# A Hymba decoder layer on one core: other step tables, five more seven-product pairs, extra buffers in two parts

## The chip, the core and the metric

The kernel runs on one core of a Trainium2 chip. The metric is the device time of one execution in microseconds (us), less being better. TensorE (PE) multiplies, VectorE (DVE) and ScalarE (ACT) split and add, GpSimd (POOL) does small work and starts some transfers, SyncE (SP) starts most of them.

## The reference

One layer over 256 tokens of width 2048, in float32. The change touches only the last three matrix products:

```python
u = rmsnorm(h, ln1_w)
...                                    # recurrent and retention heads give y
h = h + y @ w_out                      # 2048 x 2048
u = rmsnorm(h, ln2_w)
ff = silu(u @ w_gate) * (u @ w_up)     # 2048 x 5632, twice
h = h + ff @ w_down                    # 5632 x 2048
return rmsnorm(h, final_norm_w)
```

## The kernel before, in words

**Splits.** Every float32 operand is cut into a high part, a cast to float32r on ScalarE (`split`, L123), and a low part, the difference, on VectorE (L124). A product is then three matmuls, high by high, high by low and low by high (`three`, L683 to L685), each 128x128 by 128x512. Weights come by 512 KB transfers on SP's queue into `raw` tiles; the splits of one such tile are the pair `wh`, `wl` (`split_tiles`), or smaller tiles of the common pool (`bh`, `t4h`).

**Pairs.** The depth of a product is walked in pairs of 128-row tiles. A pair against a 512-column part of each side makes a 2x2 by 2x2 block product for a result in four PSUM banks, c11, c12, c21 and c22. A plain pair does it in eight products, 24 matmuls (`EIGHT`). A "summed" pair does it in seven, 21 matmuls, after Winograd: VectorE first forms four sums of the weights (`Quad.add`, L661) and four of the left side (`Left`, L546).

**Blocks.** A block is a 1024-column part of one weight matrix. Blocks 0 and 1 are `w_out`, blocks 2 to 12 are gate and up (eight pairs each), and then come two blocks of down (22 pairs each, d = 0 and 1). In blocks 0 to 12 a summed pair has two parts: the "share" (four products, 12 matmuls, done ahead during the block before, in `Block.share`, into the next block's banks) and the "direct" rest (three products, 9 matmuls, in the block itself, after a second transfer of half the weights, `Direct`). After the last share an epilogue corrects the banks: ScalarE copies c11 (L806), VectorE forms p and q (L807, L808), ScalarE writes q to c12 (L809), VectorE corrects c22 and c21 (L810, L811). Only then may the next block's plain and direct products add to these banks.

**The order of the work** is written by hand, one string per block in `STEPS`: p is a plain pair, h half of one, s a share for the block after, d a direct rest. `SUMMED` lists each block's summed pairs; `SUMMED_DOWN` and `ORDER_DOWN` do so for down, whose first three summed pairs of d = 0 are shared during block 12. A loop at the end (`AHEAD`, L1130) keeps three half-pair loads, with their splits and sums, ahead of the step that uses them. A scheduler then orders the instructions of each engine.

**Seams.** At the end of block 1, `out_post` adds the residual rows to the banks (L597), squares them on ScalarE (L598), and `turn` transposes them on TensorE into four banks (`ht`, L588), which ScalarE scales into `hf` (L591) and splits (`Left`). The rows are saved to DRAM (`kept_rows`) and read back for down, where `down_post` multiplies them by the final norm's weight `fw` (L984) and writes the output.

**Buffers.** There are six `raw` and four split tiles. From block 3 to block 12 the space of the residual rows is lent to two more of each (`raw2`, `split2`); `swap_back` returns it at the start of down and loads the eight rows and `fw` at once on GpSimd's queue.

Of the kernel before, what the change touches and what calls it, by code (L numbers as in the profile page):

```python
# [14 lines left out]
P = 128  # L15
# [27 lines left out]

@with_exitstack
def tile_hymba_layer(ctx: ExitStack, tc: tile.TileContext, A: dict, out: bass.AP):
# [2 lines left out]

    cpool = ctx.enter_context(tc.tile_pool(name="consts", bufs=1))
    apool = ctx.enter_context(tc.tile_pool(name="acts", bufs=60))  # L50
    rpool = ctx.enter_context(tc.tile_pool(name="raw", bufs=6))
    wpool = ctx.enter_context(tc.tile_pool(name="split", bufs=4))
    early = ctx.enter_context(ExitStack())
    xpool = early.enter_context(tc.tile_pool(name="resid", bufs=8))
    epool = early.enter_context(tc.tile_pool(name="conv", bufs=2))
    tpool = early.enter_context(tc.tile_pool(name="tmp", bufs=6))
    late, resid, more, turn_of = [], [xpool], [], [0, 0]
    extra = ExitStack()
# [5 lines left out]
    def nm(s):  # L64
        counter[0] += 1
        return f"{s}_{counter[0]}"

    def act_tile(name, dt=F32):
        return apool.tile([P, 512], dt, tag="act", name=nm(name))
# [2 lines left out]
        return resid[0].tile([P, 512], dt, tag="xh", name=nm(name))  # L72

    def split_tiles():
        turn_of[1] += 1
        pool_ = more[1] if more and turn_of[1] % 3 == 0 else wpool
        return [pool_.tile([P, 1024], F32R, tag=g, name=nm(g)) for g in ("wh", "wl")]

    def raw_tile():
        turn_of[0] += 1  # L80
        pool_ = more[0] if more and turn_of[0] % 4 == 0 else rpool
        return pool_.tile([P, 1024], F32, tag="raw", name=nm("raw"))

    def late_tile(name, dt=F32):
        return late[0].tile([P, 512], dt, tag="late", name=nm(name))
# [40 lines left out]
    class Unit:  # L126
# [113 lines left out]
    def defer(steps, f):  # L240
        later.append([steps, f])
# [305 lines left out]
    class Left:  # L547
# [3 lines left out]

        names = ("a11", "a21", "a12", "a22", "s1", "s2", "s3", "s4")

        def __init__(self, f, sums):
            self.h, self.l = [act_tile("ah", F32R)], [act_tile("al", F32R)]
            split(self.h[0], self.l[0], f)
            if sums:
                a11, a21, a12, a22 = (f[:, n * P : n * P + P] for n in range(4))
                g = act_tile("s")
                s1, s2, s3, s4 = (g[:, n * P : n * P + P] for n in range(4))  # L560
                v.tensor_tensor(out=s1, in0=a22, in1=a21, op=ALU.subtract)
                v.tensor_tensor(out=s2, in0=a11, in1=s1, op=ALU.add)
                v.tensor_tensor(out=s3, in0=a11, in1=a21, op=ALU.subtract)
                v.tensor_tensor(out=s4, in0=a12, in1=s2, op=ALU.subtract)
                self.h.append(act_tile("sh", F32R))
                self.l.append(act_tile("sl", F32R))
                split(self.h[1], self.l[1], g)

        def __getitem__(self, which):
# [117 lines left out]
    def block(index, quads, lefts, post, ps, tail, early={}, ordered=False):  # L687
# [214 lines left out]

    def make_left(p):
        if dl[p] is None:
            dl[p] = Left(ff[p], p in EARLY_DOWN + SUMMED_DOWN[0] + SUMMED_DOWN[1])

    def down_block(d, ahead):
        ps = {} if d else ahead.ps
# [63 lines left out]
    def down_post(cb, t, c0, cw, src=None):  # L972

        h = htok[(cb, t)][:, c0 : c0 + cw]
        src = h if src is None else src
        f = fw[cb][:, c0 : c0 + cw]
# [126 lines left out]
    def stop_more():  # L1103
        more.clear()

    def swap_back():
        extra.close()
        late.append(ctx.enter_context(tc.tile_pool(name="late", bufs=4)))
        resid[0] = ctx.enter_context(tc.tile_pool(name="resid2", bufs=8))
        for key in [(cb, t) for cb in range(4) for t in range(2)]:  # L1110
# [8 lines left out]
    ]  # L1119
    down = Block(NB + 2, lambda i: A["w_down"][i], dl, None, "", EARLY_DOWN, make_left)  # L1120
    for b, after in zip(blocks, blocks[1:] + [down]):
        if b.index == 3:
            program.append(([], swap))
        if b.index == NB + 1:
            program.append(([], stop_more))
        b.put(after)
    program.append(([], swap_back))

    for d in range(2):
        down_block(d, down)  # L1130
# [117 lines left out]
```

## Time and profile before

| | before |
| --- | --- |
| median of three runs | 1083.56 us (1082.75 to 1084.05) |
| the profiled execution | 1082.46 us |
| its span | 1080.7 us (1.76 us lie outside it) |
| TensorE matmuls | 1070.2 us busy, 5089 instructions |
| TensorE weight loads | 897.7 us busy |
| VectorE | 964.1 us busy, 1399 instructions |
| ScalarE | 664.5 us busy, 947 instructions |
| GpSimd | 57.2 us busy, 73 instructions |

Busy times are of the span. A matmul row shows 0.39 us, but matmuls overlap, so what counts is the distance from one start to the next. "Idle before" and the waits name what ended an engine's idle time; idle time of an engine that nobody waits for costs nothing.

### The profile page before, as it was taken

The numbers are of one execution on the slowest core, as the hardware profiler recorded it, in microseconds if no ns is written. First come the engines' busy times: TensorE is split into PE (matmuls) and PEld (weight loads), VectorE is DVE, ScalarE is ACT, GpSimd is POOL, SyncE is SP. The second block draws the span as 40 slices with busy tenths as digits, with TensorE's granted clock in tenths as the row PEclk, the third lists the DMA queues.
The fourth block names the chain that finished last, engine by engine and source line by source line (L and its number), as shares of the span: only waits on it lengthen the run. The fifth ranks groups of instructions, "written<-read, shape, count | busy, mean of one in ns | idle before, by whom it ended". The sixth has DMA issues, their size and how long they took to land.

```text
span 1080.7 us, 14590 instructions
## 1 busy us (share of the span) xinstructions
PE 1070.2 (99%) x5089; PEld 897.7 (83%) x5089; DVE 964.1 (89%) x1399; ACT 664.5 (61%) x947; POOL 57.2 (5%) x73
## 2 busy tenths in 40 slices
PE   9999999999999999999999999999999999999997
PEld 7888888888888888888888888888888888888886
DVE  7889789988878889989999999999999889997886
ACT  7666644468756676656656565665656656654563
POOL 0602230000000000000000000000002000000001
PEclk9999999999999999999999999999999999999999
DMA  9965475554556588677776777777767856474662
GB/s 325 336 213 171 159 254 166 183 176 158 192 195 234 183 304 273 231 235 256 257 270 228 251 260 242 263 269 232 258 234 270 289 181 214 162 245 159 214 212 101
DMA packets 71386, 244.62 MB, mean 226 GB/s; under 512 B 8208, under 2 KB 8592, under 8 KB 71312
## 3 DMA queue, kind: packets, MB, share of 16 engines
q1 hardware_dynamic: 68400, 236.34, 64.6%
q0 software_dynamic: 1472, 4.72, 1.3%
q10 hardware_dynamic: 1440, 2.62, 0.6%
q8 instruction: 40, 0.66, 0.2%
q14 instruction: 34, 0.28, 0.1%
HBM read 239.46 MB, written 4.19 MB: 225 GB/s over the span
## 4 chain that ended last, share of the span: by engine, by line
PE 98%; DVE 1%; DMA 1%; POOL 0%; SPq 0%; ACT 0%; issue 0%; POOLq 0%; ACTq 0%
PE c L685 22%; PE c L683 22%; PE c L684 22%; PE fm L194 11%; PE fm L196 5%; PE tm L174 3%; PE tm L175 3%; PE tm L176 3%; PE p L683 1%; PE p L685 1%; PE p L684 1%; PE ft L865 1%; DMA x<-in_x 1%; PE ht L588 0%; PE sc L492 0%; DVE wl L124 0%
## 5 line engine op out<-in xcount | busy, mean ns | idle before, releaser
L123 ACT CAST wh<-raw 128x1024 fp32r<-128x1024 f32 (+1 forms) x498 | 462.9, 959 | 323.8 <-PE c L685 130.8
L124 DVE TENSOR_TENSOR wl<-raw,wh 128x1024 fp32r<-128x1024 f32 (+1 forms) x498 | 542.2, 1115 | 72.5 <-ACT wh L123 71.2
L684 PE MATMUL c<-wl,ah 128*128 128x512 f32 x826 | 322.7, 391 | 0.0
L685 PE MATMUL c<-wh,al 128*128 128x512 f32 x826 | 321.8, 390 | 0.0
L683 PE MATMUL c<-wh,ah 128*128 128x512 f32 x826 | 280.3, 391 | 0.0
L683 PEld LDWEIGHTS c<-wh,ah 128*128 128x128 f32 x826 | 155.1, 188 | 32.0 <-ACT wh L123 0.3
L685 PEld LDWEIGHTS c<-wh,al 128*128 128x128 f32 x826 | 155.2, 188 | 31.8
L684 PEld LDWEIGHTS c<-wl,ah 128*128 128x128 f32 x826 | 155.2, 188 | 31.6
L194 PE MATMUL fm<-u,wh 128*128 128x512 f32 x512 | 161.4, 396 | 0.0
L196 PEld LDWEIGHTS fm<-u,wl 128*128 128x128 f32 x512 | 96.1, 188 | 22.4
L196 PE MATMUL fm<-u,wl 128*128 128x256 f32 x512 | 101.2, 279 | 0.0
L661 DVE TENSOR_TENSOR raw<-raw,raw 128x512 f32<-128x512 f32 x114 | 78.4, 689 | 2.0
L661 DVE TENSOR_TENSOR raw<-raw 128x512 f32<-128x512 f32 x114 | 78.3, 688 | 1.4
L194 PEld LDWEIGHTS fm<-u,wh 128*128 128x128 f32 x512 | 78.4, 189 | 0.3
L684 PE MATMUL c<-wl,sh 128*128 128x512 f32 x192 | 74.3, 390 | 0.0
L685 PE MATMUL c<-wh,sl 128*128 128x512 f32 x192 | 73.7, 390 | 0.0
L683 PE MATMUL c<-wh,sh 128*128 128x512 f32 x192 | 67.3, 391 | 0.3 <-ACT sh L123 0.3
L176 PE MATMUL tm<-wh,u 128*128 128x512 f32 x128 | 48.7, 391 | 0.0
L175 PE MATMUL tm<-wl,u 128*128 128x512 f32 x128 | 48.7, 393 | 0.0
L174 PE MATMUL tm<-wh,u 128*128 128x512 f32 x128 | 46.9, 394 | 1.4 <-ACT u L298 1.4
L683 PEld LDWEIGHTS c<-wh,sh 128*128 128x128 f32 x192 | 36.1, 188 | 8.1 <-ACT sh L123 0.7
L685 PEld LDWEIGHTS c<-wh,sl 128*128 128x128 f32 x192 | 36.1, 188 | 7.5
(247 smaller groups left out, 1027.4 us busy)
## 6 DMA issues: line engine op xcount, KB each, us to landing
raw<-in_w_gu SPq DMA_DIRECT2D x216, 512.0 KB, 5.3
raw<-in_w_down SPq DMA_DIRECT2D x91, 512.0 KB, 4.6
raw<-in_w_out SPq DMA_DIRECT2D x34, 512.0 KB, 3.7
raw<-in_w_lx SPq DMA_DIRECT2D x16, 512.0 KB, 6.4
raw<-in_w_k SPq DMA_DIRECT2D x16, 512.0 KB, 3.6
raw<-in_w_q SPq DMA_DIRECT2D x16, 512.0 KB, 4.2
raw<-in_w_rg SPq DMA_DIRECT2D x16, 512.0 KB, 3.5
raw<-in_w_lg SPq DMA_DIRECT2D x16, 512.0 KB, 3.5
```

What stands on the lines that cost most here:

```text
L123: act.copy(out=dst_h, in_=src)
L124: v.tensor_tensor(out=dst_l, in0=src, in1=dst_h.bitcast(F32), op=ALU.subtract)
L174: pe.matmul(ps, ah, wh, start=first, stop=False)
L175: pe.matmul(ps, ah, wl, start=False, stop=False)
L176: pe.matmul(ps, al, wh, start=False, stop=last)
L194: pe.matmul(ps, wh, hl, start=n + i == 0, stop=False)
L196: pe.matmul(ps[:, :S], wl, hl[:, :S], start=False, stop=n + i == len(order) - 1)
L661: v.tensor_tensor(out=dst, in0=a, in1=b, op=ALU.add)
L683: pe.matmul(p, ah, bh, start=first, stop=False, skip_group_check=onto)
L684: pe.matmul(p, ah, bl, start=False, stop=False, skip_group_check=onto)
L685: pe.matmul(p, al, bh, start=False, stop=last, skip_group_check=onto)
L865: pe.transpose(pt[:, o : o + P], g[:, (2 * b + c) * P : (2 * b + c) * P + P], ident)
```

## The change

It has four parts.

1. **Seven products in five more pairs.** Blocks 2, 3 and 12 get one summed pair more, (2, 3) to (1, 2, 3), and (1, 2, 3) to (0, 1, 2, 3) twice. Down's block d = 1 gets two more, pairs 12 and 19 (nine instead of seven). Their left sums exist already from d = 0; `BESIDE` puts these into a small pool of their own so that they survive.
2. **Other steps.** In the strings of blocks 1, 2, 3, 11 and 12 each new share and direct rest gets a place. Down's d = 1 no longer goes through its pairs as 0, 1, 2, ... but alternates plain and summed ones from its first step on.
3. **Buffers in two parts.** One extra split tile (`split_near`) is there from block 0 until step 5 of d = 1, another with two raw tiles (`raw_far`, `split_far`) from block 3 until step 6 of d = 0. So there are 5 split tiles in blocks 0 to 2 (4 before), 6 in blocks 3 to 12 (6 before), and 6, then 5, in down (4 before).
4. **Rows return in halves.** Four of the eight rows come back after step 9 of d = 0, four after step 7 of d = 1, and `fw` after step 8 of d = 1, by `hooks` that `block` runs behind the step of that number; `down_post` looks `fw` up late for the first two column parts.

Two places show what the tables do to the queues. In these rows a name's first number is the tile's own; `c11_677` to `c22_678` are block 1's banks, `hf` and `ht` those of `turn`.

ScalarE at the end of block 1, before: the rows from the last two casts ahead of the norm's table load to the second `hf`.

```order
L123 CAST wh_829_4069<-raw_828_4067 128x1024
L258 ACT_TABLE_LOAD
L258 ACTIVATE rs1_824_4053<-v2_120,eps_t_93 128x2
L591 ACTIVATE hf_832_4086<-ht_831_4085,small_90 128x256 x2
L123 CAST ah_833_4093<-hf_832_4086 128x512
L591 ACTIVATE hf_836_4098<-ht_835_4097,small_90 128x256 x2
L123 CAST wh_848_4147<-raw_847_4145 128x512
```

The same place after the change (lines are three higher there).

```order
L126 CAST wh_834_4108<-raw_824_4044 128x1024
L126 CAST wh_839_4118<-raw_838_4116 128x1024
L261 ACT_TABLE_LOAD
L261 ACTIVATE rs1_832_4092<-v2_120,eps_t_93 128x2
L126 CAST wh_825_4046<-raw_833_4100 128x512
L126 CAST wh_858_4196<-raw_857_4194 128x1024
L126 CAST t4h_836_4112<-raw_833_4100 128x512
L126 CAST wh_861_4202<-raw_860_4200 128x512
L594 ACTIVATE hf_842_4135<-ht_841_4134,small_90 128x256 x2
L126 CAST ah_843_4142<-hf_842_4135 128x512
```

Four casts, one of 1024 and three of 512 columns, now stand between the table load and the first `hf`. On TensorE the first share for block 3, which takes the bank that this `hf` empties, comes 46 instructions behind the last matmul into c11_677 (16 of them transposes), where it came 79 behind it.

TensorE from the last share for down, in block 12, before; c12_1666 is one of down's banks, c12_1588 and its like are block 12's.

```order
L685 MATMUL c12_1666_7926<-wh_1695_8043,sl_1694_8040 128x512
L684 MATMUL c11_1585_7562<-wl_1707_8105,ah_841_4117 128x512
L685 MATMUL c11_1585_7562<-wh_1706_8104,al_842_4118 128x512
L684 MATMUL c12_1588_7574<-wl_1707_8105,ah_841_4117 128x512
L685 MATMUL c12_1588_7574<-wh_1706_8104,al_842_4118 128x512
```

The same place after: c12_1684 is down's bank, ah_1736 the left side of down's first plain pair.

```order
L688 MATMUL c12_1684_7989<-wh_1713_8106,sl_1712_8103 128x512
L686 MATMUL c12_1598_7603<-wh_1727_8173,ah_855_4178 128x512
L687 MATMUL c12_1598_7603<-wl_1728_8174,ah_855_4178 128x512
L688 MATMUL c12_1598_7603<-wh_1727_8173,al_856_4179 128x512
L686 MATMUL c12_1598_7603<-wh_1733_8200,ah_855_4178 128x512
L687 MATMUL c12_1598_7603<-wl_1734_8201,ah_855_4178 128x512
L688 MATMUL c12_1598_7603<-wh_1733_8200,al_856_4179 128x512
L686 MATMUL c11_1681_7977<-wh_1738_8219,ah_1736_8215 128x512
L687 MATMUL c11_1681_7977<-wl_1739_8220,ah_1736_8215 128x512
L686 MATMUL c12_1684_7989<-wh_1738_8219,ah_1736_8215 128x512
```

Between the last share and the first plain matmul into the same bank stood 45 matmuls, and now stand 8. On ScalarE five casts of 1024 columns now stand between the copy of c11 (L811) and the cast ah_1736, and a sixth between that and the copy into c12 (L814).

Over the whole program TensorE has 15 instructions fewer, VectorE 33 more, ScalarE 13 more and SP three more (three reloads of 512 KB for the new direct rests). The diff, cut:

```diff
-SUMMED = ((), (4, 5), (2, 3), (1, 2, 3)) + ((0, 1, 2, 3),) * 8 + ((1, 2, 3),)
+SUMMED = ((), (4, 5), (1, 2, 3)) + ((0, 1, 2, 3),) * 10
...
-STEPS = ("pppspppspp", "ppspdpsdpp", "pdpsdpspspp", "pspsdpsdpsdp") + ("psdhsdhsdhsdhp",) * 7 + ("psdpsdpsddp", "psdpsdpsdpp")
+STEPS = ("pppspppspp", "ppspdpspsdp", "pspsdpsdpsdp") + ("psdhsdhsdhsdhp",) * 9 + ("psdpsdpsddp",)
...
-SUMMED_DOWN = (9, 12, 15, 17, 19), (5, 7, 9, 11, 13, 15, 17)
-ORDER_DOWN = (3, 4, 0, 5, 6, 1, 7, 8, 2) + tuple(range(9, 22)), tuple(range(22))
+SUMMED_DOWN = (9, 12, 15, 17, 19), (5, 7, 9, 11, 12, 13, 15, 17, 19)
+ORDER_DOWN = (3, 4, 0, 5, 6, 1, 7, 8, 2) + tuple(range(9, 22)), (0, 12, 1, 19, 2, 5, 3, 7, 4, 9, 6, 11, 8, 13, 10, 15, 14, 17, 16, 18, 20, 21)
+BESIDE = (12, 19)
...
     def split_tiles():
-        turn_of[1] += 1
-        pool_ = more[1] if more and turn_of[1] % 3 == 0 else wpool
-        return [pool_.tile([P, 1024], F32R, tag=g, name=nm(g)) for g in ("wh", "wl")]
+        counts[0] += 1
+        n = counts[0] % (4 + len(more_split))
+        p = more_split[n - 4] if n >= 4 else wpool
+        return [p.tile([P, 1024], F32R, tag=g, name=nm(g)) for g in ("wh", "wl")]
...
         for i in range(n):
             program.append(([quads[i]], step(i)))
+            if i in hooks[ordered]:
+                program.append(([], hooks[ordered][i]))
...
-                defer(13 + 2 * cb + t, lambda: v.tensor_tensor(out=h, in0=h, in1=f, op=ALU.mult))
+                defer(13 + 2 * cb + t, lambda: v.tensor_tensor(out=h, in0=h, in1=fw[cb], op=ALU.mult))
...
+    def near_begins():
         early.close()
-        more.append(extra.enter_context(tc.tile_pool(name="raw2", bufs=2)))
-        more.append(extra.enter_context(tc.tile_pool(name="split2", bufs=2)))
+        more_split.append(near.enter_context(tc.tile_pool(name="split_near", bufs=1, reuse_waits="tile")))
...
+    def near_ends():
+        near.close()
+        late.append(ctx.enter_context(tc.tile_pool(name="late", bufs=4, reuse_waits="tile")))
+        load_fw()
...
+    def far_begins():
+        kept_stack.close()
+        more_split.append(
+            far.enter_context(tc.tile_pool(name="split_far", bufs=1, side="right", reuse_waits="tile"))
+        )
+        more_raw.append(
+            far.enter_context(tc.tile_pool(name="raw_far", bufs=2, side="right", reuse_waits="tile"))
+        )
...
+    def rows_back(d):
+        resid[0] = ctx.enter_context(tc.tile_pool(name=f"resid_{d}", bufs=4, side="right", reuse_waits="tile"))
+        for key in [(cb, t) for cb in (2 * d, 2 * d + 1) for t in range(2)]:
             htok[key] = res_tile("htok")
             pool.dma_start(out=htok[key], in_=kept[key])
-        load_fw()
...
+    hooks = {0: {6: far_stops, 9: far_ends}, 1: {5: near_stops, 8: near_ends, 7: sums_end}}
```

More of the change, by code (lines that the diff above doesn't have):

```diff
@@ L50, in tile_hymba_layer @@
     apool = ctx.enter_context(tc.tile_pool(name="acts", bufs=60))
+    kept_stack = ctx.enter_context(ExitStack())
+    xpool = kept_stack.enter_context(tc.tile_pool(name="resid", bufs=8, side="right"))
     rpool = ctx.enter_context(tc.tile_pool(name="raw", bufs=6))
@@ L53, in tile_hymba_layer @@
     early = ctx.enter_context(ExitStack())
-    xpool = early.enter_context(tc.tile_pool(name="resid", bufs=8))
     epool = early.enter_context(tc.tile_pool(name="conv", bufs=2))
     tpool = early.enter_context(tc.tile_pool(name="tmp", bufs=6))
-    late, resid, more, turn_of = [], [xpool], [], [0, 0]
-    extra = ExitStack()
+    late, resid = [], [xpool]
+    more_raw, more_split, counts = [], [], [0, 0]
     pmm = ctx.enter_context(tc.tile_pool(name="pmm", bufs=4, space=PSUM))
@@ L74, in split_tiles @@
     def split_tiles():
-        turn_of[1] += 1
-        pool_ = more[1] if more and turn_of[1] % 3 == 0 else wpool
-        return [pool_.tile([P, 1024], F32R, tag=g, name=nm(g)) for g in ("wh", "wl")]
+        counts[0] += 1
+        n = counts[0] % (4 + len(more_split))
+        p = more_split[n - 4] if n >= 4 else wpool
+        return [p.tile([P, 1024], F32R, tag=g, name=nm(g)) for g in ("wh", "wl")]
     def raw_tile():
-        turn_of[0] += 1
-        pool_ = more[0] if more and turn_of[0] % 4 == 0 else rpool
-        return pool_.tile([P, 1024], F32, tag="raw", name=nm("raw"))
+        counts[1] += 1
+        p = more_raw[0] if more_raw and counts[1] % 4 == 0 else rpool
+        return p.tile([P, 1024], F32, tag="raw", name=nm("raw"))
     def late_tile(name, dt=F32):
@@ L552, in tile_hymba_layer, with __init__ @@
         names = ("a11", "a21", "a12", "a22", "s1", "s2", "s3", "s4")
-        def __init__(self, f, sums):
+        def __init__(self, f, sums, place=act_tile):
             self.h, self.l = [act_tile("ah", F32R)], [act_tile("al", F32R)]
@@ L564, in __init__ @@
                 v.tensor_tensor(out=s4, in0=a12, in1=s2, op=ALU.subtract)
-                self.h.append(act_tile("sh", F32R))
-                self.l.append(act_tile("sl", F32R))
+                self.h.append(place("sh", F32R))
+                self.l.append(place("sl", F32R))
                 split(self.h[1], self.l[1], g)
@@ L904, in make_left @@
         if dl[p] is None:
-            dl[p] = Left(ff[p], p in EARLY_DOWN + SUMMED_DOWN[0] + SUMMED_DOWN[1])
+            place = sum_tile if p in BESIDE else act_tile
+            dl[p] = Left(ff[p], p in EARLY_DOWN + SUMMED_DOWN[0] + SUMMED_DOWN[1], place)
     def down_block(d, ahead):
@@ L975, in down_post @@
         src = h if src is None else src
-        f = fw[cb][:, c0 : c0 + cw]
+        f = None if cb < 2 else fw[cb][:, c0 : c0 + cw]
         n = cb + (c0 > 0)
@@ L1095, in tile_hymba_layer, with near_stops, far_stops, sum_tile @@
         fm_tile(Unit(A["w_lg"][n]), u, range(KT), lambda ps, n=n: lru_out(n, ps))
-    def swap():
+    near, far = ExitStack(), ExitStack()
+    def near_begins():
         early.close()
-        more.append(extra.enter_context(tc.tile_pool(name="raw2", bufs=2)))
-        more.append(extra.enter_context(tc.tile_pool(name="split2", bufs=2)))
[L1103 to L1110, printed above, removed]
+        more_split.append(near.enter_context(tc.tile_pool(name="split_near", bufs=1, reuse_waits="tile")))
+    def near_stops():
+        more_split.clear()
+    def near_ends():
[10 more added lines that the diff above has]
+        )
+    def far_stops():
+        more_split.pop()
+        more_raw.clear()
+    beside, sums_kept = ExitStack(), []
+    def sum_tile(name, dt):
+        return sums_kept[0].tile([P, 512], dt, tag="sum", name=nm(name))
+    def rows_back(d):
+        resid[0] = ctx.enter_context(tc.tile_pool(name=f"resid_{d}", bufs=4, side="right", reuse_waits="tile"))
+        for key in [(cb, t) for cb in (2 * d, 2 * d + 1) for t in range(2)]:
             htok[key] = res_tile("htok")
             pool.dma_start(out=htok[key], in_=kept[key])
-        load_fw()
+    def far_ends():
+        far.close()
+        rows_back(0)
+        sums_kept.append(
+            beside.enter_context(tc.tile_pool(name="sums", bufs=4, side="right", reuse_waits="tile"))
+        )
+    def sums_end():
+        beside.close()
+        rows_back(1)
+    hooks = {0: {6: far_stops, 9: far_ends}, 1: {5: near_stops, 8: near_ends, 7: sums_end}}
     blocks = [Block(d, lambda i, d=d: A["w_out"][8 * d + i], y, out_post(d), STEPS[d], SUMMED[d]) for d in range(2)]
@@ L1121, in tile_hymba_layer @@
     for b, after in zip(blocks, blocks[1:] + [down]):
+        if b.index == 0:
+            program.append(([], near_begins))
         if b.index == 3:
-            program.append(([], swap))
-        if b.index == NB + 1:
-            program.append(([], stop_more))
+            program.append(([], far_begins))
         b.put(after)
-    program.append(([], swap_back))
     for d in range(2):
```

## The prediction

> **What bounds the kernel now.** I read the page first: busy times and the chain that ended last.
>
> ```profile
> span 1080.7 us, 14590 instructions
> ...
> PE 1070.2 (99%) x5089; PEld 897.7 (83%) x5089; DVE 964.1 (89%) x1399; ACT 664.5 (61%) x947; POOL 57.2 (5%) x73
> ...
> PE 98%; DVE 1%; DMA 1%; POOL 0%; SPq 0%; ACT 0%; issue 0%; POOLq 0%; ACTq 0%
> ```
>
> The chain lies on TensorE for 98%. Whether it is at its pace the timeline tells (start, time from first start to last end, line, count), and the windows (start:end, length, busy us and count of PE, PEld, DVE, ACT, POOL, then PEclk, DMA share, GB/s).
>
> ```profile
> 842.54 1.07 PE L683 MATMUL c<-wh,ah 128*128 128x512 f32 x4
> 840.50 0.39 PE L685 MATMUL c<-wh,sl 128*128 128x512 f32 x1
> ```
>
> ```profile
> 338.00:384.00 46.00, 45.70 (x209) 37.52 (x208) 40.84 (x62) 30.71 (x49) 0.00 (x0) 1.00 0.64 214
> 384.00:433.00 49.00, 49.00 (x225) 40.67 (x225) 43.64 (x59) 35.19 (x54) 0.00 (x0) 1.00 0.83 281
> 433.00:478.00 45.00, 45.00 (x204) 37.34 (x203) 41.31 (x52) 27.99 (x38) 0.00 (x0) 1.00 0.72 243
> 500.00:600.00 100.00, 100.00 (x451) 82.97 (x450) 95.16 (x120) 60.43 (x79) 0.00 (x0) 1.00 0.76 255
> 769.00:813.00 44.00, 44.00 (x199) 36.50 (x199) 40.23 (x54) 27.79 (x39) 1.76 (x4) 1.00 0.64 218
> 813.00:851.00 38.00, 38.00 (x173) 31.49 (x173) 35.79 (x51) 24.94 (x34) 4.63 (x9) 1.00 0.90 319
> 960.00:984.00 24.00, 24.00 (x107) 19.89 (x106) 19.23 (x24) 11.43 (x17) 0.00 (x0) 1.00 0.53 176
> ```
>
> Four starts with the last end after 1.07 us, one matmul being 0.39: starts lie (1.07 − 0.39) / 3 = 0.227 us apart. These windows are roughly blocks 1, 2 and 3, a steady stretch, blocks 11 and 12, and the head of down's d = 1. PE is busy throughout in all but the first. So a matmul less is worth 0.227 us. But VectorE works 95.16 of 100 us in the steady stretch, close behind.
>
> What waits for buffers is seen in the waits (us in total, times, longest), of the whole span and of the window of block 1:
>
> ```profile
> ACT wh L123 <- PE c L685: 130.8, 88, 4.3
> ```
>
> ```profile
> PEld c L683 <- ACT sh L123: 0.7, 1, 0.7
> ```
>
> ScalarE waits 130.8 us for TensorE to free split tiles, but TensorE waits for a split only once, 0.7 us. So extra split tiles gain at most that by themselves; they are cover for what follows.
>
> **What the change saves.** Five pairs with 21 matmuls instead of 24: 15 × 0.227 = 3.4 us off the path.
>
> **What it adds to VectorE.** Its pace in a crowded place (start and time as above):
>
> ```profile
> 605.49 2.35 DVE L124 TENSOR_TENSOR wl<-raw,wh 128x1024 fp32r<-128x1024 f32 x2
> 607.76 0.69 DVE L661 TENSOR_TENSOR raw<-raw 128x512 f32<-128x512 f32 x1
> 608.36 1.29 DVE L124 TENSOR_TENSOR wl<-raw,wh 128x512 fp32r<-128x512 f32 x2
> 609.57 0.69 DVE L124 TENSOR_TENSOR t4l<-raw,t4h 128x512 fp32r<-128x512 f32 x1
> ```
>
> By starts, a 1024-column split takes 2.27 / 2 = 1.135 us, a 512-column one 1.21 / 2 = 0.605, a sum 0.60. A share (s) takes 4 × 0.60 + 3 × 0.605 + 1.135 = 5.35 us of VectorE and 12 matmuls = 2.72 us of TensorE; a direct rest (d) 1.135 and 2.04; a plain pair (p) 2.27 and 5.45. So s and d for p is +4.2 us of VectorE, three times. In down a summed pair needs 4 × 0.60 + 0.605 + 3 × 1.135 = 6.4, +4.1, twice. Together about 20.9 us more.
>
> Set into the strings (VectorE against TensorE, us):
> - block 1, one s more: 40.84 + 5.35 = 46.2 of 46 + 2.72 = 48.7;
> - block 2, s and d for p: 47.8 of 48.3, which is 99%;
> - block 3, d for p: 40.2 of 41.6;
> - block 11, one s more: 45.6 of 46.7;
> - block 12, d for p: 34.7 of 34.6, full.
>
> So hardly any of VectorE's time is left over there, and I see four places where TensorE will stand.
>
> **A, the head of block 2.** The timeline before, by engine:
>
> ```profile
> 384.04 0.39 PE L685 MATMUL c<-wh,al 128*128 128x512 f32 x1
> 391.06 0.27 PE L588 MATMUL ht<-ident,htok 128*128 128x128 f32 x1
> 391.41 0.93 PE L588 MATMUL ht<-ident,htok 128*128 128x128 f32 x7
> 400.15 0.39 PE L683 MATMUL c<-wh,ah 128*128 128x512 f32 x1
> ```
>
> ```profile
> 385.19 0.63 ACT L598 ACTIVATE junk<-htok 128x512 f32<-128x512 f32 x1 [0.31 <-DVE htok L597]
> 387.27 1.05 ACT L123 CAST wh<-raw 128x1024 fp32r<-128x1024 f32 x1 [0.74 <-ACT junk L598]
> 392.01 0.82 ACT L591 ACTIVATE hf<-ht,small 128x256 f32<-128x256 f32 x2
> 398.95 1.56 ACT L123 CAST wh<-raw 128x1024 fp32r<-128x1024 f32 x2
> 846.42 0.58 ACT L809 COPY c<-q 128x512 f32<-128x512 f32 x1
> ```
>
> The first row is the last matmul into block 1's c11, the fourth the first share for block 3. It needs the bank of the first `ht`, free when `hf` ends at 392.83, 8.8 us after the first row; the share came 16.1 us after it, 7.3 us to spare. With block 2's string beginning p, s instead of p, d, p, s, only 46 instructions lie between: 30 × 0.227 + 16 transposes × (0.93 − 0.27) / 6 = 8.6 us. And ScalarE has four casts more ahead of `hf`, one of 1024 and three of 512 columns: of the 1.56 us pair 1.04 and 0.52, so 2.6 us. So 8.8 + 2.6 − 8.6 = 2.8 us of standing. ScalarE idled 0.31 + 0.74 us there, which may take some back: 1.7 at least. Above, block 2's epilogue now falls into the same stretch, since its third share is two steps from block 1's end: its copy (0.58) and three sums (1.8) stand among the row additions and casts, so up to 5.2. I take 4.5, since both queues hold that work ahead of `hf`.
>
> **B, VectorE without reserve in blocks 1 to 3, 11 and 12.** Its waits for ScalarE in the windows of block 2, 11 and 12, in this order:
>
> ```profile
> DVE wl L124 <- ACT wh L123: 2.9, 7, 0.6
> ```
>
> ```profile
> DVE wl L124 <- ACT wh L123: 3.2, 2, 1.9
> ```
>
> ```profile
> DVE wl L124 <- ACT wh L123: 1.1, 3, 0.6
> ```
>
> If these waits stay, 2.9 exceeds block 2's room of 0.5 by 2.4, and 4.3 the 1.0 of blocks 11 and 12 by 3.3: 5.7 us. If three loads of run-ahead and the extra split tile cover all, 0. The steady stretch shows 95.2% without a pause; 98 to 100% is nearer the upper end: 3.5.
>
> **C, from block 12 to down.** The epilogue before, on VectorE:
>
> ```profile
> 841.18 0.69 DVE L807 TENSOR_TENSOR p<-c,p 128x512 f32<-128x512 f32 x1
> 844.04 0.68 DVE L808 TENSOR_TENSOR q<-p,c 128x512 f32<-128x512 f32 x1
> ```
>
> The last share started at 840.50, and the copy to c12 ended at 847.00, 6.5 us later. The first plain matmul into c12 came 46 starts behind the share, 10.4 us, with 3.9 to spare. Now s, d, d, p ends the block where s, d, p, p did, with one p taken away from behind the last share, and it comes 9 starts behind: 2.0 us. At worst 6.5 − 2.0 = 4.5 us. Done bare, the chain is 0.39 + 0.69 + 0.68 + 0.58 = 2.3, at least 0.3. ScalarE now has six casts of 1024 columns ahead of that copy, and VectorE is full: 4.0.
>
> **D, the head of down's d = 1.** Its first four steps were p, p, p, p and become p, s, p, s: VectorE + 8.3. The four multiplications by `fw` leave this stretch for later, − 2.4. So 19.2 + 5.9 = 25.1 us in 24 − 6 × 0.227 = 22.6: 2.5 short, less the loads done ahead. `fw` and the rows are now loaded behind hooks; transfers, with KB and us to landing:
>
> ```profile
> raw<-in_w_gu SPq DMA_DIRECT2D x216, 512.0 KB, 5.3
> htok<-kept_rows POOLq DMA_DIRECT2D x8, 256.0 KB, 8.1
> fw<-in_final_norm_w POOLq DMA_DIRECT2D x4, 256.0 KB, 5.8
> ```
>
> The rows have some ten steps, about 50 us, before the first sum needs them: 8.1 is hidden. The three reloads of weights are issued three loads ahead, and 5.3 is hidden too, as for the others. The multiplications by `fw` stand on VectorE a step or two behind its load, with the next pairs' sums and splits queued behind them. If all of 5.8 were waited for, that is the upper end; the lower is 0. I take 2.0, mostly the shortage.
>
> **Sum.** 4.5 + 3.5 + 4.0 + 2.0 = 14.0, less 3.4: +10.6. The profiled execution took 1082.46 us, so 1093.1; the median of before lies 1.1 above it, so the forecast is **1094.2**. With all lower ends (1.7 + 0 + 0.3 + 0) it is 1082.2, with all upper (5.2 + 5.7 + 4.5 + 5.8) 1101.4.
>
> **Rivals**, from the median 1083.56:
> 1. *The cover holds, so faster.* If ScalarE and VectorE clear A to D out of turn early enough, as the 7.3 and 3.9 us to spare show they do now, only the saving is left: **1080.2**. It decides where A stands under 3.4 us and nothing else does. Against it: the order of both queues is fixed, and A's count of 46 leaves too little by any row.
> 2. *Only A is paid.* The extra split tile covers the rest: 4.5 − 3.4 = +1.1, **1084.7**. For it: TensorE waited for a split once in the whole program. Against it: C's 9 starts.
> 3. *The clock falls during A.* The windows behind the last matmul:
>
> ```profile
> 1070.00:1074.00 4.00, 2.97 (x24) 2.69 (x22) 3.43 (x14) 2.46 (x8) 2.61 (x3) 1.00 0.30 111
> 1074.00:1076.00 2.00, 0.00 (x0) 0.00 (x0) 1.88 (x7) 1.08 (x2) 0.26 (x2) 1.00 0.90 302
> 1076.00:1078.00 2.00, 0.00 (x0) 0.00 (x0) 0.00 (x0) 0.05 (x1) 0.00 (x0) 0.68 1.00 347
> 1078.00:1080.70 2.70, 0.00 (x0) 0.00 (x0) 0.00 (x0) 0.00 (x0) 0.00 (x0) 0.50 0.35 131
> ```
>
> Matmuls end near 1073.0; a mean of 0.68 with 0.50 behind it puts the fall at 1076 + 2 × 0.36 = 1076.7, 3.7 us later. A's 4.5 us could cross that. If the clock then takes as long to return, half speed for 3.7 us costs 1.9: **1096.1**. Against it: the fall may be tied to fixed instants, not to the pause. [...]
> 4. *VectorE is already the bound.* PEld is busy 83% and VectorE 89%, so the added 20.9 us might come on top with nothing saved: **1104.5**. Against it: starts are unbroken at 0.227 us, and VectorE idles 4.8% in the steady stretch. [...]
>
> **How the numbers follow.** Forecast 0.70, rival 1 0.11, rival 2 0.10, rival 3 0.06, rival 4 0.03. About 0.2% (2.2 us) is what a measurement of this kernel can tell from no change. Faster by more is rival 1, 0.11; within it rival 2, 0.10; slower the rest, 0.79. The range reaches from just under rival 2, 1084.0, to all upper ends, 1101; outside are rivals 1 and 4, 0.14 together.
>
> **What would show it.** In the profile after, 15 matmuls fewer at 0.227 us; gaps between PE starts near 388 us for `hf` (A), ahead of down's first pair for c12 (C), and in its second block's head for VectorE's splits (D); VectorE busy some 20 us longer. I am wrong if PE shows starts without gaps, if the gap at A is under 2 us, or if PEclk falls below 1.00 there.

## The result, and the profile after

The changed kernel takes 1112.82 us (median of four runs, 1111.15 to 1118.73) against 1083.62: 1.028 times as long, interval 1.0242 to 1.0319. That is 29 us more, above the upper end of the forecast, 1101. The profiled execution took 1113.12 us, with a span of 1111.3 instead of 1080.7: 30.6 more.

Its page, span and busy times:

```profile
span 1111.3 us, 14601 instructions
...
PE 1083.8 (98%) x5074; PEld 897.6 (81%) x5074; DVE 984.3 (89%) x1432; ACT 672.1 (60%) x960; POOL 56.5 (5%) x73
```

15 matmuls fewer, and VectorE 20.2 us busier, as forecast. But "98% busy" hides what happened, since the end of a matmul is modelled. The waits of TensorE (who waits, by what it writes, and for what; us in total, times, longest), where before had 0.3 us behind the first 300 us:

```profile
PE c L687 <- DVE wl L127: 5.5, 5, 2.4
PE c L686 <- ACT hf L594: 4.6, 1, 4.6
PE c L686 <- ACT wh L126: 2.1, 2, 1.9
PE c L686 <- ACT ah L126: 2.0, 1, 2.0
PE p L686 <- ACT wh L126: 1.5, 2, 1.0
PE c L686 <- ACT c L814: 1.2, 3, 0.5
PE p L687 <- DVE wl L127: 1.1, 1, 1.1
```

They come to 18.0 us. The windows show where, and a second loss beside them (start:end, length, busy us and count of PE, PEld, DVE, ACT, POOL, then PEclk):

```profile
394.10:399.10 5.00, 0.41 (x2) 0.00 (x0) 4.40 (x7) 4.96 (x9) 0.00 (x0) 1.00 0.69 223
399.10:403.10 4.00, 3.96 (x10) 3.13 (x11) 3.97 (x10) 3.92 (x9) 0.00 (x0) 0.57 0.89 268
...
555.00:580.00 25.00, 23.18 (x97) 18.23 (x96) 20.21 (x27) 11.56 (x17) 0.00 (x0) 0.93 0.69 235
...
605.00:620.00 15.00, 12.63 (x50) 9.89 (x50) 13.81 (x18) 8.13 (x11) 0.00 (x0) 0.89 0.63 217
620.00:820.00 200.00, 200.00 (x891) 163.52 (x890) 184.19 (x233) 120.14 (x159) 0.00 (x0) 1.00 0.73 245
820.00:880.00 60.00, 54.13 (x229) 41.97 (x228) 52.13 (x75) 36.19 (x48) 0.00 (x0) 0.97 0.67 229
...
985.00:1035.00 50.00, 46.23 (x196) 35.88 (x195) 41.93 (x50) 25.61 (x33) 4.25 (x8) 1.00 0.58 202
```

TensorE stands at 394 (A), near 566 and 612 (where blocks 6 and 7 begin; before never stood there), at 828 to 833 and 860 (block 12), 871 to 875 (the seam to down, C) and at 1001 to 1031 (D). Behind four of these pauses PEclk is below 1.00: 0.57 in the 4 us behind A, 0.93, 0.89 and 0.97 in the windows of the pauses at 566, 612 and 871 to 875.

The third loss hides in the row of 620 to 820: no pause, full clock, yet 891 matmuls where before had 904 in the same 200 us:

```profile
620.00:820.00 200.00, 200.00 (x904) 165.87 (x903) 187.68 (x239) 123.53 (x164) 2.17 (x4) 1.00 0.75 251
```

The two rows hold about the same small share of transposes. Worked out from the starts of all pairs of neighbouring 512-column matmuls between 640 and 740 us, the distance is 0.2297 us, where it was 0.2269. It is 0.227 up to block 3's start, 0.229 to 0.230 from there until the far buffers end, and 0.227 to 0.228 behind that, in down.

From these starts the 30.6 us add up. What gaps exceed 0.227 us by is 24.4 us more than in before: A 4.9, blocks 6 to 12 10.2, C 3.6, D 5.7. Matmuls at half clock lose 4.5, the longer distance about 5. The saving gives back 3.4. Together 30.5.

Ahead of the pauses near 566, 612 and 1001 us stands a wait for weights. ScalarE and VectorE, from the timeline:

```profile
560.44 1.57 ACT L126 CAST wh<-raw 128x512 fp32r<-128x512 f32 x2 [4.02 <-DMA raw<-in_w_gu]
561.09 0.69 DVE L127 TENSOR_TENSOR wl<-raw,wh 128x512 fp32r<-128x512 f32 x1 [2.34 <-ACT wh L126]
```

```profile
1001.04 0.62 ACT L126 CAST bh<-raw 128x512 fp32r<-128x512 f32 x1 [5.28 <-DMA raw<-in_w_down]
1001.69 0.69 DVE L127 TENSOR_TENSOR bl<-raw,bh 128x512 fp32r<-128x512 f32 x1 [4.29 <-ACT bh L126]
```

A transfer into a `raw` tile starts when VectorE has split what the tile held. The weights that ScalarE waited for until 1001.04 were issued at 993.59, at the end of such a split. So VectorE, short of time as it is, idles 2.3 and 4.3 us here: a split that comes late brings the next weights late, and VectorE then has to catch up. Over the whole run ScalarE waits 19.2 us for gate and up weights, where it was 5.8.

### The profile page after: what moved, and what is told of

It reads as the page before. It is cut to its first block, busy times and chain, and to the rows that moved or that the text cites. A ratio compares the mean times of both kernels' runs of the same rounds, so it can differ in the third digit from the quotient of the medians.

```text
span 1111.3 us, 14601 instructions
## 1 busy us (share of the span) xinstructions
PE 1083.8 (98%) x5074; PEld 897.6 (81%) x5074; DVE 984.3 (89%) x1432; ACT 672.1 (60%) x960; POOL 56.5 (5%) x73
## 5 line engine op out<-in xcount | busy, mean ns | idle before, releaser
L127 DVE TENSOR_TENSOR wl<-raw,wh 128x1024 fp32r<-128x1024 f32 (+1 forms) x506 | 548.9, 1109 | 84.7 <-ACT wh L126 83.4
L687 PE MATMUL c<-wl,ah 128*128 128x512 f32 x796 | 313.4, 395 | 5.6 <-DVE wl L127 5.5
L688 PE MATMUL c<-wh,al 128*128 128x512 f32 x796 | 309.5, 392 | 0.0
L688 PEld LDWEIGHTS c<-wh,al 128*128 128x128 f32 x796 | 150.0, 188 | 32.0
L664 DVE TENSOR_TENSOR raw<-raw,raw 128x512 f32<-128x512 f32 x124 | 85.1, 687 | 1.9
L664 DVE TENSOR_TENSOR raw<-raw 128x512 f32<-128x512 f32 x124 | 84.9, 686 | 1.3
L687 PE MATMUL c<-wl,sh 128*128 128x512 f32 x206 | 80.5, 392 | 0.0
L688 PE MATMUL c<-wh,sl 128*128 128x512 f32 x206 | 80.0, 391 | 0.0
L686 PE MATMUL c<-wh,sh 128*128 128x512 f32 x206 | 72.7, 396 | 0.0
L1141 POOL DMA_DIRECT2D htok<-kept_rows x8 | 4.3, 545 | 832.8 <-DVE wl L127 729.4
```

Source lines behind the costliest of these rows:

```text
L127: v.tensor_tensor(out=dst_l, in0=src, in1=dst_h.bitcast(F32), op=ALU.subtract)
L664: v.tensor_tensor(out=dst, in0=a, in1=b, op=ALU.add)
L686: pe.matmul(p, ah, bh, start=first, stop=False, skip_group_check=onto)
L687: pe.matmul(p, ah, bl, start=False, stop=False, skip_group_check=onto)
L688: pe.matmul(p, al, bh, start=False, stop=last, skip_group_check=onto)
```

## The experiments

The theory after the result: the pauses are VectorE's and ScalarE's shortage that the prediction named (A to D), and the longer distance comes from where the new right-hand tiles lie. Tiles of the kernel before all begin at multiples of 128 bytes of a partition; the right-hand pools (rows, `raw_far`, `split_far`, `sums`) begin 32 bytes off. The rival for the distance: more crowded engines and transfers. The rival for the pauses: the buffers, not the added products. All kernels here compute the whole layer. Ratios are to the kernel before, run beside them.

**e1_aligned.**

```diff
+    even = ctx.enter_context(tc.tile_pool(name="even", bufs=1, side="right"))
+    even.tile([P, 8], F32, name="even_pad")
     xpool = kept_stack.enter_context(tc.tile_pool(name="resid", bufs=8, side="right"))
```

> The changed kernel with 32 bytes set aside at the right end of SBUF, so that the tiles of the right-hand pools (raw_far, split_far, the rows) begin at multiples of 64 bytes; nothing else differs. Theory (the 32-byte offset of those tiles slows matmuls): in the stretch 640 to 820 us the mean distance of matmul starts falls from 0.2297 to 0.2268 us, and the time by about 4.8 us, to 1108; the pauses stay. Rival (starts are slower because the engines and transfers are more crowded, wherever the tiles lie): distance and time stay, 1112.8 within 1.5.

Measured 1112.74 us, ratio 1.0274 (1.0259 to 1.0289): no change, and the row of 620 to 820 is as before the edit.

```profile
620.00:820.00 200.00, 200.00 (x891) 164.01 (x891) 185.60 (x234) 120.98 (x160) 0.00 (x0) 1.00 0.74 249
```

The theory fails in this form. But these 32 bytes bring the tiles only to odd multiples of 64.

**e2_before_odd.** The kernel before, with everything behind the activations shifted by 32 bytes:

```diff
+    odd = ctx.enter_context(tc.tile_pool(name="odd", bufs=1))
+    odd.tile([P, 8], F32, name="odd_pad")
     rpool = ctx.enter_context(tc.tile_pool(name="raw", bufs=6))
```

> The kernel before with 32 bytes set aside ahead of the raw and split tiles, so that all of these begin at odd multiples of 32 bytes. Theory (the offset slows each matmul that streams such a tile, by 5 to 9 ns): some 4,800 matmuls, so 24 to 43 us more, 1108 to 1127. Rival (crowding): 1083.6 within 1.

Measured 1106.96, ratio 1.0223 (1.0206 to 1.0240): 24 us for 32 bytes.

```profile
620.00:820.00 200.00, 200.00 (x880) 161.32 (x879) 183.04 (x229) 120.49 (x159) 0.00 (x0) 1.00 0.74 246
```

880 matmuls for 904; by starts, 0.2331 us apart instead of 0.2268. TensorE waits for no split more than before and the clock is 1.00, and the instructions stand in the order of before on all five engines, but for one save of a row that ScalarE starts a few places later, so this is no crowding. In this run it costs matmul time where the tiles begin, 6.3 ns from start to start.

**e5_aligned_128.** As e1, with `[P, 24]`, 96 bytes, for `[P, 8]`.

> The changed kernel with 96 bytes set aside at the right end instead of 32, so that the right-hand tiles begin at multiples of 128 bytes, as every tile of the kernel before does. Theory (tiles that begin off a multiple of 128 slow the matmuls around them): matmul starts 0.2268 us apart between 640 and 820 us, where they were 0.2297, and the time about 5 us lower, 1108. Rival (it is the place at the right end, or crowding): 1112.8 within 1.5, starts 0.229 apart.

Measured 1108.77, ratio 1.0236 (1.0221 to 1.0252), 4 us less than the changed kernel:

```profile
620.00:820.00 200.00, 200.00 (x900) 165.49 (x898) 185.35 (x234) 121.19 (x161) 0.00 (x0) 1.00 0.74 248
```

By starts the distance is 0.2269 between 640 and 740 us. The instructions stand in the same order on all five engines as in the changed kernel and in e1. So the third loss is shown: right-hand tiles off a multiple of 128 bytes, with 891 matmuls in the 200 us whether 32 bytes off (the changed kernel) or 64 (e1), and 900 here. The pauses stay, a little longer. All kernels from here on but e3 and e4 have this padding.

**e3_buffers_only.** The changed kernel with the four tables of before, and `BESIDE` empty:

```diff
-SUMMED = ((), (4, 5), (1, 2, 3)) + ((0, 1, 2, 3),) * 10
+SUMMED = ((), (4, 5), (2, 3), (1, 2, 3)) + ((0, 1, 2, 3),) * 8 + ((1, 2, 3),)
...
-BESIDE = (12, 19)
+BESIDE = ()
```

> The changed kernel with the tables of before (SUMMED, STEPS, SUMMED_DOWN, ORDER_DOWN, and no sums kept beside): the buffers in two parts and the rows in halves alone. Theory of the prediction (extra buffers neither gain nor cost) and the offset's price: 1083.6 + 4.8 = 1088, no pause of TensorE over 0.5 us. Rival (the new rotation over pools makes TensorE stand by itself): pauses of 5 us or more in all, 1093 or more.

Measured 1103.12, ratio 1.0184 (1.0169 to 1.0199): two thirds of the loss without one added product. TensorE's main waits:

```profile
PE c L687 <- DVE wl L127: 3.4, 3, 2.3
PE p L686 <- ACT wh L126: 3.1, 2, 2.5
PE c L686 <- ACT wh L126: 2.0, 3, 1.6
```

They lie at 645 and 733 (steady blocks), 858, 1013 and 1038 us. The rival was right: the buffers cost by themselves.

**e4_gate_up_only.** The changed kernel with down's tables of before.

> The changed kernel with down's tables of before (no pairs 12 and 19 in seven products, order 0 to 21); gate and up as changed. Theory (D, the head of down's second block, is made by its new pairs and order): the pauses of 5.7 us at 1001 to 1031 go, 1.4 us of saving is given up: 1108.5. Rival (they come from the buffers and the late fw): 1114.

Measured 1110.71, ratio 1.0252 (1.0223 to 1.0282). D's pauses are gone, as the theory has it; but e3 has these same tables for down, and has pauses there. So neither D's pairs nor the late `fw` decide alone: what the blocks before leave behind matters, and this run does not settle D.

**e6_buffers_rotation.** e3 with the padding, and the two extra split tiles taken at other turns of six:

```diff
-        p = more_split[n - 4] if n >= 4 else wpool
+        at = (2, 5) if len(more_split) == 2 else (4,) * len(more_split)
+        p = more_split[at.index(n)] if n in at else wpool
```

> e3_buffers_only with the right-hand tiles at multiples of 128 bytes, and the two extra split tiles taken at the third and sixth split of six instead of the fifth and sixth, as the pool of two was taken before. Products, tiles and their number are the same, and each tile still waits for the sixth split before it. Theory (the buffers cost nothing by themselves; another rotation makes the scheduler lay VectorE's and ScalarE's queues in another order, and the order of e3 makes TensorE stand): the pauses of 13 us fall under 4, time 1084 to 1088. Rival (tiles in several pools, or rows that return in halves, cost by themselves): 1103 - 5 = 1098.

Measured 1088.63, ratio 1.0048 (1.0031 to 1.0065). Tiles, products and the distance of six between two uses of a tile are those of e3, and 14 us are gone, of which the padding accounts for about 4 to 5. What differs besides is the order in which the scheduler laid the queues: a comparison with e3 has 292 differing lines for VectorE's some 1,400 instructions and 972 for TensorE's 5,000. TensorE's waits in front of matmuls into the `c` banks nearly vanish:

```profile
PE p L689 <- ACT wh L129: 1.7, 3, 0.7
...
PE c L691 <- DVE al L130: 1.0, 1, 1.0
PE c L689 <- ACT wh L129: 0.6, 3, 0.2
```

ScalarE's waits for gate and up weights fall from 18.9 us in e3 to 10.2. With 95 of 100 us of VectorE in use in the steady blocks (before), it seems that the order of its queue decides whether TensorE stands. That it is the order is argued: e3 with the padding alone was not run (in the changed kernel the padding alone left the pauses, e5), and which instructions decide it was not traced. What is left, 5 us, lies in one pause of 1.1 at 852 and in 4.5 us of small ones between 980 and 1030.

**e9_fw_early.** e6 with the near tile given up earlier, so that `fw` comes before the second block:

```diff
-    hooks = {0: {6: far_stops, 9: far_ends}, 1: {5: near_stops, 8: near_ends, 7: sums_end}}
+    hooks = {0: {6: far_stops, 9: far_ends, 11: near_stops, 14: near_ends}, 1: {7: sums_end}}
```

> e6_buffers_rotation with the near split tile given up in down's first block (steps 11 and 14 instead of 5 and 8 of the second), so that fw is loaded before the second block begins and its four multiplications can stand at that block's head again, as before. Theory (the pauses of about 4.5 us between 980 and 1030 come from the multiplications and the late fw, now among the seven-product pairs where VectorE has no room): 1088.6 - 4 = 1084.6. Rival (they come from the queue order as such, or from raw and split tiles): 1088.6 within 1.5.

Measured 1084.40, ratio 1.0003 (0.9993 to 1.0012): the kernel before. On VectorE the multiplications by `fw` had stood among the seven-product pairs in e6:

```profile
994.73 1.28 DVE L993 TENSOR_TENSOR htok<-htok,fw 128x512 f32<-128x512 f32 x2
997.07 1.28 DVE L993 TENSOR_TENSOR htok<-htok,fw 128x512 f32<-128x512 f32 x2
```

and now stand at the block's head, with its plain pairs:

```profile
962.86 1.29 DVE L993 TENSOR_TENSOR htok<-htok,fw 128x512 f32<-128x512 f32 x2
964.67 0.68 DVE L993 TENSOR_TENSOR htok<-htok,fw 128x512 f32<-128x512 f32 x1
967.61 0.69 DVE L993 TENSOR_TENSOR htok<-htok,fw 128x512 f32<-128x512 f32 x1
```

Behind 980 us no gap is left. The edit also takes the fifth split tile from some sixteen steps, the last ten of down's first block and the first six of its second, which evidently costs nothing. With tiles, rotation and `fw` mended, the whole rearrangement of buffers is worth nothing either way.

**e7_after_rotation.** The changed kernel with padding and e6's rotation.

> The changed kernel with both edits: right-hand tiles at multiples of 128 bytes and the extra split tiles at the third and sixth split of six. Theory (A and C follow from the steps, most of B from the queue order): A's pause of 4.8 and C's of about 4 stay, those at 560 and 612 us (5.5 with the half clock behind them) go: 1108 - 6 = 1102. Rival (B is VectorE's load in itself): 1108.

Measured 1103.85, ratio 1.0192 (1.0176 to 1.0208), between the theory's 1102 and the rival's 1108 and nearer the theory. The pauses at 560 and 612 are gone; A (4.8) and C (3.0 and 1.1) stay; new small ones stand at 471 and behind 980.

**e8_head_undone.** e5 with block 2's string changed:

```diff
-STEPS = ("pppspppspp", "ppspdpspsdp", "pspsdpsdpsdp") + ("psdhsdhsdhsdhp",) * 9 + ("psdpsdpsddp",)
+STEPS = ("pppspppspp", "ppspdpspsdp", "pdpsdpsdspsp") + ("psdhsdhsdhsdhp",) * 9 + ("psdpsdpsddp",)
```

> The changed kernel with right-hand tiles at multiples of 128 bytes and block 2's string pdpsdpsdspsp instead of pspsdpsdpsdp: the same pairs in seven products, but the direct rest and a plain pair stand again between the first plain pair and the first share. Theory (A is the share that follows the first plain pair at once): the pause of 4.8 us and its half clock (1.6) go, 1108 - 6.4 = 1101.6, if nothing else moves. Rival (VectorE is short around there anyway, and the pause moves on): still 1108, with pauses elsewhere in blocks 2 and 3.

Measured 1117.58, ratio 1.0309 (1.0294 to 1.0325): slower still. The wait for `hf` is gone, but the rival was right beyond what it said: pauses of 5.7 and 3.9 us stand at 438 and 444 us, at the seam of blocks 2 and 3, where the string now ends s, p, s, p.

```profile
PE c L688 <- ACT wh L128: 9.0, 7, 5.5
PE c L689 <- DVE wl L129: 5.0, 4, 2.0
PE c L688 <- ACT c L816: 4.5, 4, 3.3
```

**e10_pairs_2_3**, **e11_pair_12** and **e12_pairs_down**: e6 with one part of the new tables each.

> e6_buffers_rotation with the changed tables of blocks 1 to 3 alone (two more pairs in seven products there, 6 matmuls less). Theory (A): a pause of 4.8 us near 394 with about 2 of half clock, less 1.4: 1088.6 + 5.4 = 1094. Rival (A needs the other changes too): 1087.2.

> e6_buffers_rotation with the changed tables of blocks 11 and 12 alone (one more pair in seven products, 3 matmuls less). Theory (C, VectorE full in block 12): pauses between 820 and 880 of 6 us instead of 1.3 and up to 2 of half clock, less 0.7: 1088.6 + 6 = 1094.6. Rival (C comes from what blocks 1 to 3 left behind): 1088.

> e6_buffers_rotation with down's changed tables alone (pairs 12 and 19 of the second block in seven products, the new order, their sums kept beside; 6 matmuls less). Theory (D, VectorE's added 8.2 us): pauses of 5 us more behind 950, less 1.4: 1088.6 + 3.7 = 1092.3. Rival (the new order spreads the work, and D was the buffers' part alone): 1087.2.

| e6 and | matmuls less | measured | ratio | against e6 |
| --- | --- | --- | --- | --- |
| nothing | 0 | 1088.63 | 1.0048 (1.0031 to 1.0065) | |
| pairs of blocks 2, 3 | 6 | 1089.14 | 1.0047 (1.0032 to 1.0062) | none |
| pair of block 12 | 3 | 1096.17 | 1.0111 (1.0093 to 1.0129) | +0.0063, about 7 us |
| pairs 12, 19 of down | 6 | 1090.11 | 1.0062 (1.0047 to 1.0077) | +0.0014, within the intervals |

e10 has A in full:

```profile
399.55 0.80 PE L689 MATMUL c<-wh,ah 128*128 128x512 f32 x1 [4.68 <-ACT hf L597]
```

and half clock behind it (its mean granted clock is 0.997, e6's 0.998); yet its time is e6's, because the pauses behind 980 us shrank from 4.5 to 1.1 and that at 852 went. In e11 block 12's one pair, saving 0.7 us, costs 7. Its waits:

```profile
PE c L689 <- ACT ah L129: 2.2, 1, 2.2
PE p L689 <- ACT wh L129: 2.1, 1, 2.1
PE c L689 <- DVE c L818: 1.5, 1, 1.5
```

The first and third of these are the seam to down, 2.2 and 1.5 us at 851 to 857, with half clock behind them (the run's mean granted clock is 0.992). So C comes from the tables of blocks 11 and 12, not from what blocks 1 to 3 left behind. But the 7 us are not C alone: the second wait ends at 904, in down's first block, in 3.3 us of gaps with half clock behind them again, while those behind 980 shrank from 4.5 to 0.5.

**e13_share_early.** e9 with the pairs of blocks 2 and 3, and block 1's shares earlier than in the change:

```diff
-STEPS = ("pppspppspp", "ppspdpspsdp", "pspsdpsdpsdp") + ...
+STEPS = ("pppspppspp", "ppspspdpsdp", "pspsdpsdpsdp") + ...
```

> e9_fw_early with the pairs of blocks 2 and 3 in seven products as changed (6 matmuls less), block 2's string pspsdpsdpsdp as changed, but block 1's string ppspspdpsdp instead of ppspdpspsdp: its second share stands two steps earlier, so the scheduler has block 2's last share and epilogue further from the seam. Theory (A needs that epilogue among the row additions and casts): the pause at 394 falls from 4.8 us to about 1 and no half clock follows: 1084.4 - 1.4 + 2.5 = 1085.5. Rival (the share right behind block 2's first plain pair makes the pause by itself): 4.8 and a half clock of 1.2 stay, with 1.2 behind them, 1084.4 + 5.8 = 1090.2.

Measured 1087.98, ratio 1.0047 (1.0032 to 1.0062). The wait for `hf` is gone although block 2 still begins p, s; in its place TensorE waits once for the row additions:

```profile
391.58 1.09 PE L594 MATMUL ht<-ident,htok 128*128 128x128 f32 x8 [0.86 <-DVE htok L603]
```

No half clock follows: the run's mean granted clock is 0.998, that of before. So the share behind the first plain pair does not make A by itself; it takes block 2's epilogue in the same stretch, as the upper end of A had it. The changed kernel agrees: ScalarE waits 2.5 us there for the q of that epilogue, and the row additions start only behind it. But the 4.8 us do not come back: small pauses at 361, 363, 467 and 524 us add up to what A was, 5.7 us of gaps in all, and the ratio is 0.0044 above e9's, some 4.7 us.

**e14_down_fw_early.** e9 with down's changed tables.

> e9_fw_early with down's changed tables (pairs 12 and 19 in seven products, the new order, 6 matmuls less). Theory (what is left of D is VectorE's added 8.2 us, early fw or not): pauses of 3 to 4 us behind 950: 1084.4 - 1.4 + 3.5 = 1086.5. Rival (with fw early the new order spreads the load and nothing waits): 1083.0.

Measured 1089.58, ratio 1.0056 (1.0039 to 1.0072): 6.3 us more than before, against the theory's 2.1. Pauses at 967 to 970 (2.5) and 992 (1.9), with half clock behind the first (mean granted clock 0.996), as TensorE waits for `bh` and `wh`:

```profile
PE p L689 <- ACT bh L129: 2.3, 2, 1.7
...
PE p L689 <- ACT wh L129: 0.7, 1, 0.7
```

So the new pairs do cost in down, once the multiplications by `fw` and the first steps p, s, p, s share the head. With `fw` late they hardly do: e12, the same steps with `fw` late, has 1.0062 against e14's 1.0056. Set side by side, `fw` early gains 0.0045 with the old steps (e6, e9) and 0.0006, nothing, with the new ones (e12, e14); and the new steps cost 0.0053 with `fw` early and 0.0014, nothing clear, with `fw` late. Either burden costs some 5 to 6 us at this place, and both together no more.

No version here beats the kernel before; e9 equals it. Since each added part that was tried costs at least what it saves, no mixture of them was run.

## Why the prediction was wrong

**The direction held, the size did not, and the mechanism only in part.** Four places were named, and TensorE stood at all four, but not everywhere for the reason given; the sum of +10.6 became 29.2. The 14.0 us of pauses became 24.4, and two losses that the sum did not have, the clock and the matmul itself, added 9.5.

**The saving**, 15 × 0.227 = 3.4: the page has 15 matmuls fewer. Right.

**A**, 4.5: the wait for `hf` at 399.14 is 4.6 us, the gap 4.8. Right in place and size, and e13 supports the cause that the upper end named, the epilogue among the row additions.

```profile
394.13 0.39 PE L688 MATMUL c<-wh,al 128*128 128x512 f32 x1
399.14 0.50 PE L686 MATMUL c<-wh,ah 128*128 128x512 f32 x1 [4.62 <-ACT hf L594]
```

**B**, 3.5 with 5.7 at most: 10.2 us of gaps in blocks 6 to 12. The step that failed is "extra split tiles gain at most that by themselves; they are cover for what follows". It treated buffers as something that can only take waits away. e3 shows 20 us of loss with no product added, 4 to 5 of them from where the tiles lie and most of the rest pauses. With another rotation over the same six tiles, which gives the queues another order, and with the padding, 5 are left (e6): it is not the number of buffers that costs. How a late split grows into a pause the rows at 560 and 561 show: the weights are fetched late, and ScalarE and VectorE idle for them. The bound of 5.7 was made of waits in blocks 2, 11 and 12 of the old order; the pauses at 566 and 612 lie in blocks whose strings did not change and which the prediction did not look at, because they ran without a pause before.

**C**, 4.0: 3.6 us of gaps at 871 to 876. Right in place and size, and e11 shows that block 12's pair makes it. The longer wait is not the one that was named: TensorE waits 2.0 us for `ah`, the left side of down's first pair, and then 0.5 for c12.

```profile
873.83 0.55 PE L686 MATMUL c<-wh,ah 128*128 128x512 f32 x1 [1.96 <-ACT ah L126]
875.26 0.79 PE L686 MATMUL c<-wh,ah 128*128 128x512 f32 x1 [0.46 <-ACT c L814]
```

Both `ah` and the copy to c12 stand on ScalarE behind the same row of casts, so by these rows the second wait would have lasted longer without the first.

**D**, 2.0 with 5.8 at most: 5.7. VectorE's shortage at the head, the cause named first, is there, but it acts through the loads that the prediction held for hidden. Between 982 and 989 us VectorE has the row additions and four of the new sums in its queue ahead of the next 1024-column split; SP waits 9.4 us, until 990.4, for that split to free a `raw` tile, and the weights come late, at 1001. The size was taken from the shortage alone. The upper end meets the 5.7 by luck: it stood for a wait for `fw`, and there is none. "The four multiplications by `fw` leave this stretch for later, − 2.4" was a credit that gained nothing. In the changed kernel they stand behind the pauses of 1001 to 1008:

```profile
1025.74 1.29 DVE L990 TENSOR_TENSOR htok<-htok,fw 128x512 f32<-128x512 f32 x2
1028.68 1.29 DVE L990 TENSOR_TENSOR htok<-htok,fw 128x512 f32<-128x512 f32 x2
```

With the old steps the late place costs 4 to 5 us, where they stand among seven-product pairs (e9 against e6); with the new steps early or late makes no difference (e12, e14).

**The clock**, a rival with 0.06 and one pause in mind: it happened, behind four pauses, for 3.413 us each, and cost 4.5. At A it is 0.57, which the prediction itself had named as a sign of being wrong. Only A was thought long enough, since 3.7 us lay between the last matmul and the fall; a pause of 2.5 us at 612 was enough. The point against this rival, that the fall may be tied to fixed instants, fits the changed kernel, whose falls lie 50, 13 and 76 times 3.413 us apart (last section), but it speaks for more falls as much as for fewer.

**The matmul itself**: that 0.227 us per matmul holds after the change was assumed without a word. The right-hand pools put tiles 32 bytes off multiples of 128 bytes, and that cost 4 to 5 us (e5). No row of before could have shown it; the address of the new tiles could have been compared with the old ones.

**The other rivals**: "the cover holds" and "only A is paid" fail by the pauses above. "VectorE is already the bound" would give 20.9; VectorE's busy time rose by 20.2, but it works 184 of 200 us between 620 and 820 and idles, waiting for weights, ahead of the pauses, so it is not a bound all along. It binds in places.

The parts do not add up: on e6's base they cost 0, 7 and 1.5 us apart, and some 15.6 together (1.0192 against 1.0048). Why one order of the same work leaves pauses and another none stays open: e3 and e6 differ by rotation and padding alone, but which pair of instructions decides was not found.

## What to carry to other kernels

VectorE worked 95.16 of 100 us in the steady blocks, beside a TensorE without a pause, and there added work could not be priced by its microseconds alone: the buffers in two parts cost 20 us with no product added (e3), and 5 with the padding and another rotation over the same tiles (e6). Look at what such work sets free, here the tiles that the next weights go into. Try a buffer change alone, with the old work, before putting new work on it. Where a step is moved, price the place where it arrives; and when pools are moved, look at where their tiles begin, down to the byte: 32 bytes cost 24 us in e2.

## What the runs showed of the hardware that was not expected

**Matmul starts lay further apart where tiles began off multiples of 128 bytes.** With all raw and split tiles 32 bytes off, starts of 128x512 matmuls lie 0.2331 us apart instead of 0.2268 (e2: 880 matmuls in the 200 us from 620, for 904); with one of six pairs of split tiles 32 bytes off, 0.2297 on the mean (the changed kernel: 891), and with it 64 off as many matmuls (e1: 891); at multiples of 128 bytes 0.2269 (e5: 900). Other offsets were not run. Splits on VectorE and casts on ScalarE took no longer in the changed kernel than in before (1.218 against 1.221 us; 1.050 against 1.052 us, means of 1024 columns behind 290 us). In the changed kernel 189 of 421 distances between 640 and 740 us are 0.229 or more (18 in before), far more than one pair of tiles in six can account for, so some of them lie at matmuls that read other tiles; why was not tested.

**The half clock came in stretches of 3.413 us, and a pause of 2.5 us was enough for one.** A pause of the changed kernel, with what follows:

```profile
612.20:614.90 2.70, 0.34 (x2) 0.00 (x0) 2.70 (x5) 2.70 (x5) 0.00 (x0) 0.97 0.87 302
614.90:618.00 3.10, 3.09 (x9) 2.40 (x9) 3.10 (x6) 0.93 (x2) 0.00 (x0) 0.50 0.72 237
618.00:621.00 3.00, 3.00 (x18) 2.51 (x17) 2.24 (x2) 0.05 (x1) 0.00 (x0) 0.98 0.63 234
```

Starts lie at 612.15 and 614.91 us, 2.5 us more than the usual distance, and the clock is 0.50 for 3.4 us. By the trace's clock records the four falls of the changed kernel stand at 399.69, 570.36, 614.73 and 874.14 us, which is 50, 13 and 76 times 3.413 us from one to the next, and the half clock behind each of the four lasts 3.413 us. The length of a pause alone did not decide whether the clock fell. In e1 and in e5 TensorE waits at the same place for the same cast. For each, the matmul that ends the pause, then the windows:

```profile
857.88 0.56 PE L688 MATMUL c<-wh,ah 128*128 128x512 f32 x1 [1.80 <-ACT wh L128]
```

```profile
855.70:858.20 2.50, 0.70 (x3) 0.30 (x2) 2.47 (x4) 2.36 (x3) 0.00 (x0) 1.00 0.95 313
858.20:861.60 3.40, 3.40 (x9) 2.64 (x8) 2.29 (x3) 1.16 (x3) 0.00 (x0) 0.50 0.92 294
```

```profile
858.87 0.50 PE L688 MATMUL c<-wh,ah 128*128 128x512 f32 x1 [2.80 <-ACT wh L128]
```

```profile
855.70:859.30 3.60, 0.80 (x4) 0.38 (x3) 2.60 (x4) 2.47 (x4) 0.00 (x0) 1.00 0.97 340
859.30:862.70 3.40, 3.40 (x17) 2.76 (x16) 2.17 (x3) 1.04 (x3) 0.00 (x0) 1.00 0.89 310
```

In e1 the clock was 0.50 behind 1.8 us of waiting; in e5 it was 1.00 behind 2.8 us. That the 2.8 us were split over two stretches is an inference; the rows do not show where a stretch of e5 begins. With the stretches laid over the changed kernel from its falls, the four ahead of a fall hold 0.55, 1.60, 1.22 and 1.45 us of matmul time, so none of them is idle all through. The emptiest that full clock follows hold 1.66 us (from 392.86) and 1.93 (from 1003.85).
